# Sum of reciprocals on one core: another command list and a zeroed statistics tile

## The chip, the cores and the metric

The kernel runs on 1 core of one Trainium2 chip. The metric is the device time of one execution in microseconds (us); the median of the runs counts. In the text PE is TensorE, ACT is ScalarE, DVE is VectorE, POOL is GpSimd and SP is SyncE, the names that the profile uses.

## The reference

```python
x = np.abs(np.random.randn(32, 512, 1024)).astype(np.float32) + 1e-6

def reference(x):
    return np.sum(1.0 / x, axis=-1).astype(np.float32)
```

There are 32 x 512 = 16384 sums of 1024 reciprocals each, and 67.1 MB to read.

## The kernel before

Each of the 128 partitions holds 128 of the 16384 sums. A "row" u in the kernel is one of these for all partitions at once: a tile of 128 x 1024 numbers, 512 KB. Rows 0 to 126 are whole; row 127 comes in two halves, the pieces 127 and 128. The input goes through `ring`, a buffer of 46 rows in SBUF; row u lies at place u mod 46, so row 46 can be loaded when row 0 is done with.

The work is written out by hand as a list of commands, `PLAN`. Each engine does its commands in the order in which they stand there; between engines, `note` keeps track of who must wait for whom, row by row. A command is a letter, a row, "+n" for n rows in one instruction, and "@b" for a slot or a bank:

- D n: SP issues the loads of the next n rows (one load, or more at a border of the ring or of the input). It waits until the places in the ring are free.
- A u+n: ACT takes the reciprocal square root of n rows in place. The square of that is the reciprocal, and the sum of the squares is what is wanted.
- The squares are summed in one of several ways. Z: ACT squares and sums (an activation and the reading of its accumulator). Q: DVE squares and sums in one instruction. G and T: POOL squares n rows in place, DVE sums n rows. C and T: ACT squares, DVE sums. B: DVE takes statistics of each half row (count, mean and count times variance, of even and odd numbers); two later commands, K on ACT (the means squared, times the count) and M on DVE (adding up), make sums of them for many rows at once.
- P, U, L, E, R are a way of their own for one row, by pairs: 1/a + 1/b = (a + b) / (a b). P: POOL multiplies the row's two halves into a slot of `prod`. U: PE adds the halves in a bank of PSUM. L and E: ACT takes the reciprocal square root of the products, and squares it. R: DVE multiplies by the sums and adds up.
- O: SP issues six stores of the sums; a last one stands at the end of the program.

Sums go to the tile `sums`, but the statistics of the B rows go to the tile `stats`, which holds only the rows of `STATS` (11 rows from 43 in steps of 3, 18 rows from 80 in steps of 2). K0 and M0 treat the first group, K1 and M1 the second, and M writes its results into `sums` among the others. POOL has 13 idle words (`EARLY`) ahead of its first command.

The list of before has 25 loads; the first four ask for 2, 12, 12 and 9 rows.

Of the kernel before, what the change touches and what calls it, by code (L numbers as in the profile page):

```python
# [11 lines left out]
def kernel(  # L12
# [17 lines left out]
    STATS = ((43, 3, 11), (80, 2, 18),)  # L30
# [3 lines left out]

    PLAN = """
        D2 D12 D12 D9 D11 A0+2 Z0 A2 A3 A4+3 G1+3 A7 A8 A9 G6+3 A10 T1 A11+3 T2+2 Z4 Z5 G9 Z10
        Z12 G11 T6+4 D10 A14 A15+2 G13 A17+3 G16 T11 T13 A20+4 G17 Q15 G19 T16+2 A24+2 G20 A26
        A27 G21 A28+2 G23+3 A30+2 T19+3 A32+3 Z14 D8 G26 C33 Z18 G27 Z22 Z29 G28 A35+2 G30+3
        T23+6 D8 A37+3 A40+4 G34+2 T30+2 A44+2 Z36 T32 G40 Z37 T33+3 D8 Z38 G44+2 U53@0 A46+2
        T40 A48 Q42 G47 A49 A50+3 B43 T44 P53@0 T45 A54+2 G50 B46 L53 T47 Z39 D6 B49 A56+6 T50
        B52 Q54 B55 A62+2 G57 Q56 E53 G60 Z41 D6 R53 Z48 T57 A64+6 B58 G62 T60 G63 B61 T62+2
        A70+2 G65+2 B64 Z51 D7 D6 B67 Z59 D5 G68+2 A72 T65+2 D4 A73+4 B70 G71+2 T68+2 D3 A77+2
        B73 A79 G78 T71+2 D2 K0 U81@1 A80 A82+2 G79 M0 B80 A84 U85@2 B82 P81@1 Z74 D2 T78+2 Z75
        G83 L81 Z76 D2 P85@2 B84 U89@3 A86+3 T83 P89@3 U91@4 P91@4 L85 B86 G87 L89 A90 B88 L91  # L50
        T87 E81 E85 E89 R81 E91 R85 Z77 D1 D1 D1 D1 D1 D1 R89 B90 A92+2 P95@0 U95@5 R91 A94 B92
        G93 L95 B94 A96 A97 T93 A98 B96 E95 B98 Z97 P99@1 U99@6 A100+2 R95 P103@2 L99 B100 G101
        A102 U103@7 L103 B102 A104 T101 E99 E103 R99 P107@3 U107@0 A105 R103 A106 B104 P109@4
        U109@1 L107 Q105 A108 L109 B106 E107 E109 R107 P111@0 U111@2 A110 B108 A112 P113@1 R109
        U113@3 L111 B110 L113 E111 B112 E113 P115@2 U115@4 A114 R111 P116@3 L115 R113 U116@5
        E115 B114 P118@4 A117 R115 U118@6 L116 K1 Q117 L118 E116 P119@0 M1 O0 A120 U119@7 R116
        E118 Q120 L119 E119 P121@1 U121@0 R118 A122 R119 A123 Q122 L121 Q123 A124 E121 Q124 A125
        R121 A126 Q125 A127 A128 Q127 Z126 Q128
# [27 lines left out]
    stat_rows = [i for lo, step, n in STATS for i in range(lo, lo + step * n, step)]  # L86
    stats = pool.tile([P, len(stat_rows), 2, 2, 3], f32)
# [70 lines left out]
    with tc.manual_schedule():  # L158
        for _ in range(EARLY):
            nc.gpsimd.nop(hint="idle", nofuse=True)  # L160
        for op, u, n, b in (parse(tok) for tok in PLAN):
# [23 lines left out]
            elif op == "Z":  # L185
                r = place(u)[0]
                inst = nc.scalar.activation(  # L187
                    out=area(u), in_=area(u), func=Square, accum_out=sums[:, r : r + 1]
                )
                summed.add(r)  # L190
                note("ACT", inst, writes=rows(u))
# [26 lines left out]
            elif op == "R":  # L218
# [9 lines left out]
                    accum_out=sums[:, u : u + 1],  # L228
                )
                note("DVE", inst, [("bank", bank[u])], [("slot", slot[u])])  # L230
            elif op == "Q":
                r, at, w = place(u)
                joined = [u]
                while len(joined) < n:
# [4 lines left out]
                total = sums[:, r : r + 1]  # L239
# [5 lines left out]
                    scalar=total if r in summed else 0.0,  # L245
                    op0=mult,
                    op1=add,
                    accum_out=total,
                )
                summed.add(r)  # L250
                note("DVE", inst, writes=[s for i in joined for s in rows(i)])
            elif op == "B":
                i = stat_rows.index(u)
                for h in range(2):
                    inst = nc.vector.bn_stats(  # L255
                        out=stats[:, i, h], in_=ring[:, u % R, h * H : (h + 1) * H]
                    )
                    note("DVE", inst, reads=half(u, h * H), writes=[("stat", i)])
            elif op in "KM":
                lo, step, n = STATS[u]  # L260
                i = stat_rows.index(lo)
                part = stats[:, i : i + n]
                if op == "K":
                    mean = part[:, :, :, :, 1].rearrange("p f h e -> p (f h e)")
                    inst = nc.scalar.activation(  # L265
                        out=mean, in_=mean, func=Square, scale=float(H // 2) ** 0.5
                    )
                    engine = "ACT"
                else:
                    inst = nc.vector.tensor_reduce(  # L270
                        out=sums[:, lo : lo + step * (n - 1) + 1 : step],
                        in_=part[:, :, :, :, 1:].rearrange("p f h e k -> p f (h e) k"),
                        axis=mybir.AxisListType.XY,
                        op=add,
                    )
                    engine = "DVE"
                note(engine, inst, writes=[("stat", j) for j in range(i, i + n)])
# [4 lines left out]
            elif op == "T":  # L282
                inst = nc.vector.tensor_reduce(  # L283
                    out=sums[:, u : u + n],
# [4 lines left out]
                note("DVE", inst, reads=rows(u, n))  # L289
# [34 lines left out]
```

## Time and profile before

| | |
|---|---|
| median of 3 runs | 166.15 us (166.03 to 166.23) |
| span of the profiled execution, first to last instruction | 164.2 us |
| profiled execution's own time | not given apart from its span; the median stands 1.9 us above the span |
| busy: ACT, DVE, POOL, PE | 145.7, 115.9, 108.8, 38.2 us |
| instructions: ACT, DVE, POOL, PE | 148, 147, 56, 68 matmuls and as many weight loads |
| read from HBM | 67.11 MB, 409 GB/s over the span |
| PE clock granted, mean | 0.952 |

In the rows of the timeline, a group of neighbouring instructions stands with its start, the busy time of the group, engine, line, operation, what it writes and reads, the count, and in brackets how long the engine sat idle before it and what ended that. In the groups by shape there follow, after the count: busy time in us, mean duration of one in ns, and the idle time before them with its releasers. L178 is line 178: A and C; L187 is Z; L211 is L and E; L240 is Q; L220 is R; L255 is B; L265 is K; L270 is M; L280 is G; L283 is T; L194 is P; L201 is U; L170 is a load; L156 is a store.

### The profile page before, as it was taken

How to read it: one execution, taken by the hardware profiler on the slowest of the kernel's cores; microseconds unless marked ns; L12 is line 12 of the kernel's file. 1: busy time of each engine (PE TensorE's matmuls, PEld its weight loads, DVE VectorE, ACT ScalarE, POOL GpSimd, SP SyncE). 2: the span in 40 equal slices, each digit the busy share in tenths (PEclk: the TensorE clock that was granted, in tenths of full speed). 3: DMA queues.
4: the chain of work that ended last, by engine and by line, in shares of the span. 5: the costliest groups of instructions: out<-in, count | busy, mean ns of one | idle time of the engine just before them, and what ended most of it. 6: DMA issues, size and time to landing. Idle time of an engine off the chain costs nothing.

```text
span 164.2 us, 640 instructions
## 1 busy us (share of the span) xinstructions
PE 38.2 (23%) x68; PEld 14.4 (9%) x68; DVE 115.9 (71%) x147; ACT 145.7 (89%) x148; POOL 108.8 (66%) x56
## 2 busy tenths in 40 slices
PE   0000000000000000053000000065908198699700
PEld 0000000000000000020000000032302033234200
DVE  0000003559927039999999999999698969999894
ACT  3600199999999999999999999999999999999994
POOL 1000069998999999999507979999926195477300
PEclk9999999999999999999999999999975859999985
DMA  5999899899989899999998998999999999999970
GB/s 188 463 539 407 383 395 563 383 431 431 463 351 527 351 479 409 391 455 431 391 503 383 431 463 381 455 407 441 419 425 467 414 419 422 421 411 417 408 249 2
DMA packets 4611, 67.20 MB, mean 409 GB/s; under 512 B 1408, under 2 KB 1408, under 8 KB 2176
## 3 DMA queue, kind: packets, MB, share of 16 engines
q1 hardware_dynamic: 4608, 67.18, 96.3%
q14 instruction: 3, 0.02, 0.0%
HBM read 67.11 MB, written 0.07 MB: 409 GB/s over the span
## 4 chain that ended last, share of the span: by engine, by line
ACT 63%; DMA 26%; DVE 6%; issue 2%; POOL 2%; SPq 0%; DVEq 0%; POOLq 0%
ACT ring L178 47%; DMA ring<-in_x_dram 26%; ACT ring L187 10%; ACT prod L211 6%; DVE ring L240 2%; DVE stats L255 2%; POOL prod L194 2%; DVE prod L220 1%; DVE sums L283 0%; SPq L170 0%; ACT stats L265 0%; DVE sums L240 0%; DVE sums L220 0%; DVEq L240 0%; POOLq L194 0%
## 5 line engine op out<-in xcount | busy, mean ns | idle before, releaser
L178 ACT ACTIVATE ring<-ring 128x1024 f32<-128x1024 f32 (+4 forms) x65 | 104.1, 1658 | 15.2 <-DMA ring<-in_x_dram 15.1
L280 POOL TENSOR_TENSOR ring<-ring 128x1024 f32<-128x1024 f32 (+2 forms) x33 | 85.9, 2634 | 29.9 <-ACT ring L178 29.9
L283 DVE TENSOR_REDUCE sums<-ring 128x1 f32<-128x1024 f32 (+4 forms) x27 | 53.3, 1999 | 42.2 <-POOL ring L280 42.1
L201 PE MATMUL ps<-ring,ident 128*128 128x512 f32 x68 | 38.2, 712 | 117.2 <-DMA ring<-in_x_dram 115.9
L255 DVE BATCH_NORM_STATS2 stats<-ring 128x6 f32<-128x512 f32 x58 | 36.5, 679 | 3.1 <-ACT ring L178 3.1
L194 POOL TENSOR_TENSOR prod<-ring 128x512 f32<-128x512 f32 x17 | 22.5, 1339 | 15.0 <-DMA ring<-in_x_dram 10.8
L201 PEld LDWEIGHTS ps<-ring,ident 128*128 128x128 f32 x68 | 14.4, 224 | 140.2 <-POOL ring L280 71.6
L187 ACT ACTIVATE ring<-ring 128x1024 f32<-128x1024 f32 x23 | 23.9, 1041 | 0.0
L211 ACT ACTIVATE prod<-prod 128x512 f32<-128x512 f32 x34 | 19.8, 615 | 0.2
L240 DVE CUSTOM_DVE_ANT_0 ring<-ring 128x1024 f32<-128x1024 f32 (+1 forms) x12 | 17.6, 1480 | 0.5 <-ACT ring L178 0.4
L220 DVE CUSTOM_DVE_ANT_0 prod<-prod,ps 128x512 f32<-128x512 f32 x17 | 11.1, 676 | 0.1
L187 ACT ACTIVATION_READ_ACCUMULATOR ring<-ring 128x1 f32 x23 | 4.3, 187 | 0.0
L70 ACT ACT_TABLE_LOAD x1 | 1.3, 1283 | 0.7 <-PEq L308 0.7
L220 DVE DVE_READ_ACCUMULATOR2_ANT sums<- 128x1 f32 x17 | 1.4, 81 | 0.0
L240 DVE DVE_READ_ACCUMULATOR2_ANT sums<- 128x1 f32 x13 | 1.0, 81 | 0.0
L240 DVE CUSTOM_DVE_ANT_0 ring<-ring,sums 128x512 f32<-128x512 f32 x1 | 0.8, 752 | 0.1
masks.py:199 POOL TENSOR_SCALAR_AFFINE_SELECT ident<-ident 128x128 f32<-128x128 f32 x1 | 0.3, 293 | 0.5 <-POOL ident masks.py:197 0.5
L265 ACT ACTIVATE stats<-stats 128x44 f32<-128x44 f32 (+1 forms) x2 | 0.5, 272 | 0.0
L270 DVE TENSOR_REDUCE sums<-stats 128x11 f32<-128x88 f32 (+1 forms) x2 | 0.5, 264 | 0.0
masks.py:197 POOL MEMSET ident<- 128x128 f32 x1 | 0.2, 205 | 0.3 <-POOLq L308 0.3
L308 POOL MEMSET const-float32-0.0<- 128x1 f32 x1 | 0.1, 99 | 0.2 <-issue 0.2
L308 POOL MEMSET const-bfloat16-1.0<- 128x1 bf16 x1 | 0.1, 102 | 0.0
(2 smaller groups left out, 0.2 us busy)
## 6 DMA issues: line engine op xcount, KB each, us to landing
ring<-in_x_dram SPq DMA_DIRECT2D x2, 6144.0 KB, 25.8
ring<-in_x_dram SPq DMA_DIRECT2D x3, 4096.0 KB, 26.0
ring<-in_x_dram SPq DMA_DIRECT2D x3, 3072.0 KB, 26.3
ring<-in_x_dram SPq DMA_DIRECT2D x1, 5632.0 KB, 55.9
ring<-in_x_dram SPq DMA_DIRECT2D x1, 5120.0 KB, 32.4
ring<-in_x_dram SPq DMA_DIRECT2D x1, 4608.0 KB, 43.3
ring<-in_x_dram SPq DMA_DIRECT2D x4, 1024.0 KB, 37.8
ring<-in_x_dram SPq DMA_DIRECT2D x1, 3584.0 KB, 24.4
```

Source lines behind the costliest of these rows:

```text
L70: nc.scalar.add_instruction(mybir.InstLoadActFuncSet(name=nc.get_next_instruction_name(), act_func_set_id=act_sets.index("abs_reciprocal_s ...
L178: inst = nc.scalar.activation(out=area(u, n), in_=area(u, n), func=Arsqrt if op == "A" else Square, scale=FIT if op == "A" else 1.0,)
L187: inst = nc.scalar.activation(out=area(u), in_=area(u), func=Square, accum_out=sums[:, r : r + 1])
L194: inst = nc.gpsimd.tensor_tensor(out=prod[:, b], in0=ring[:, r, :H], in1=ring[:, r, H:], op=mult)
L201: inst = nc.tensor.matmul(ps[:, b], lhsT=ident, rhs=ring[:, r, h * H : (h + 1) * H], start=h == 0, stop=h == 1,)
L211: inst = nc.scalar.activation(out=pair, in_=pair, func=Arsqrt if op == "L" else Square, scale=S * FIT if op == "L" else 1.0,)
L220: inst = nc.vector.tensor_tensor_reduce(out=pair, in0=pair, in1=ps[:, bank[u]], scale=S, scalar=0.0, op0=mult, op1=add, accum_out=sums[:, ...
L240: inst = nc.vector.tensor_tensor_reduce(out=row, in0=row, in1=row, scale=1.0, scalar=total if r in summed else 0.0, op0=mult, op1=add, acc ...
L255: inst = nc.vector.bn_stats(out=stats[:, i, h], in_=ring[:, u % R, h * H : (h + 1) * H])
L265: inst = nc.scalar.activation(out=mean, in_=mean, func=Square, scale=float(H // 2) ** 0.5)
L280: inst = nc.gpsimd.tensor_tensor(out=row, in0=row, in1=row, op=mult)
L283: inst = nc.vector.tensor_reduce(out=sums[:, u : u + n], in_=area(u, n), axis=mybir.AxisListType.X, op=add,)
```

## The change

The list is another one. It has 26 loads, the first five of 10, 9, 8, 10 and 9 rows, 13 rows by pairs instead of 17, 26 B rows instead of 29, 57 rows by T instead of 47 (55 of them squared by POOL instead of 46), 24 by Z instead of 23, and 9 Q commands instead of 13. No program of an engine is to be over 152 words long. The idle words of POOL are gone.

`stats` now has a place of 12 numbers for each of the rows 0 to 118, and POOL sets it to zero at the start. A row below 119 leaves its sum there, whatever the way: B its twelve numbers, and Z, Q, T and R one number in a place that M adds up. K and M run over all rows of a block (0 to 61, 62 to 118), so that M writes `sums` for every row of the block. Rows from 119 on go to `sums` as before.

```diff
--- before.py
+++ after.py
@@ -18,7 +18,6 @@
     nc = tc.nc
     f32 = mybir.dt.float32
     P = 128
-    EARLY = 13
     D = 1024
     H = D // 2
     F = 128
@@ -27,35 +26,27 @@
     NP = 5
     PIECES = ((127, 0, 512), (127, 512, 512))
     NR = 127
-    STATS = ((43, 3, 11), (80, 2, 18),)
+    BLOCKS = (62, 119,)
     STORES = (0, 21, 43, 64, 81, 99, 116)
     S = float(2**17)
     FIT = 1.0 - 2.0**-17
     PLAN = """
-        D2 D12 D12 D9 D11 A0+2 Z0 A2 A3 A4+3 G1+3 A7 A8 A9 G6+3 A10 T1 A11+3 T2+2 Z4 Z5 G9 Z10
...
+        D10 D9 D8 D10 D9 A0+8 A8+2 G6 Z4 G2 Z5 G0+2 A10 A11+8 G8+2 Z10 G18 Z7 G12 Z13 T18
+        A20 G14+3 A24+3 Z26 A19 A21+3 T14+3 Z11 G22+4 Z20 T12 T1+2 A35 A36 T8+2 A27+7 B3 G19
+        T6 T0 G35 B21 D9 A34 G32 T22+4 C33+2 A37 Z17 G36+2 A38+8 B31 D9 T32+4 G27+4 T19 D8
+        Z45 Z38 A47+8 G39 T27+4 G40+2 T36+2 D6 G42 Z49 G52+3 A46 T39+4 Z48 Z46 A59 A60 B43
+        D8 A61+3 G59+2 T52+3 A55+4 G62 B63 B61 G44 Z56 B47 T62 G50+2 A69+2 T59+2 A64+5 B57
+        G69 G55 Z68 B64 G70 A71+7 B58 T44 G65 T50+2 D6 G66 T55 D5 B67 D6 K0 G72 Z74 D4 D4 M0
+        Z75 B76 G71 Z73 T72 A80+2 G77 T65+2 A82 G80+2 T77 D3 A78+2 T71 A83+3 T69+2 T80+2 D2
+        A90+2 G84+2 D3 D2 B82 A86+4 B79 G91 B78 Z88 B89 D2 P93@0 U93@0 A94+3 T91 G83 B86 L93
+        U92@1 P92@1 T83+3 Z96 G95 L92 Z90 E93 G94 B87 E92 A100+3 D1 U98@2 R93 P99@2 R92
+        T94+2 P98@3 L99 U99@3 E99 P97@4 L98 B100 E98 L97 U97@4 D1 P105@0 B102 A106 R98
+        P103@1 L105 U105@5 B106 A104 G101 E97 R99 L103 U103@6 R97 E105 B104 E103 D1 P108@2
+        A109+2 U107@7 R103 T101 P107@3 L108 B110 E108 G109 L107 E107 R105 D1 U111@0 A112+2
+        R107 P111@4 T109 L111 Q112 D1 A114+2 U108@1 Q113 E111 R108 Z114 B115 A117 D1 P116@0
+        U116@2 R111 A118 B117 L116 B118 E116 P119@1 A120 U119@3 R116 K1 Q120 L119 E119
+        U122@4 A121 P122@2 M1 O0 R119 A123 Q121 L122 Q123 A124 E122 Q124 A125 R122 A126 Q125
+        A127 A128 Q127 Z126 Q128
     """.split()
 
     Arsqrt = mybir.ActivationFunctionType.Abs_reciprocal_sqrt
@@ -83,8 +74,7 @@
     ring = pool.tile([P, R, D], f32)
     sums = pool.tile([P, F], f32)
     prod = pool.tile([P, NP, H], f32)
-    stat_rows = [i for lo, step, n in STATS for i in range(lo, lo + step * n, step)]
-    stats = pool.tile([P, len(stat_rows), 2, 2, 3], f32)
+    stats = pool.tile([P, BLOCKS[-1], 2, 2, 3], f32)
     ident = pool.tile([P, P], f32)
     ps = pspool.tile([P, 8, H], f32)
     make_identity(nc, ident)
@@ -138,6 +128,14 @@
                     (inst, *entry, writing, sum(count.values()), known)
                 )
 
+    def total(u, n=1):
+        if u < BLOCKS[-1]:
+            return stats[:, u : u + n, 0, 0, 2]
+        return sums[:, u : u + n]
+
+    def result(u, n=1):
+        return [("sum", i) for i in range(u, u + n)]
+
     def rows(u, n=1):
         spaces = []
         for r, at, w in (place(i) for i in range(u, u + n)):
@@ -156,8 +154,7 @@
         nc.sync.dma_start(out=out_v[a, :, at : at + hi - lo], in_=sums[:, lo:hi])
 
     with tc.manual_schedule():
-        for _ in range(EARLY):
-            nc.gpsimd.nop(hint="idle", nofuse=True)
+        note("POOL", nc.gpsimd.memset(stats, 0.0), writes=result(0, BLOCKS[-1]))
         for op, u, n, b in (parse(tok) for tok in PLAN):
             if op == "D":
                 n, u = u, loaded
@@ -185,10 +182,10 @@
             elif op == "Z":
                 r = place(u)[0]
                 inst = nc.scalar.activation(
-                    out=area(u), in_=area(u), func=Square, accum_out=sums[:, r : r + 1]
+                    out=area(u), in_=area(u), func=Square, accum_out=total(r)
                 )
                 summed.add(r)
-                note("ACT", inst, writes=rows(u))
+                note("ACT", inst, writes=rows(u) + result(r))
             elif op == "P":
                 slot[u], r = b, u % R
                 inst = nc.gpsimd.tensor_tensor(
@@ -225,9 +222,9 @@
                     scalar=0.0,
                     op0=mult,
                     op1=add,
-                    accum_out=sums[:, u : u + 1],
-                )
-                note("DVE", inst, [("bank", bank[u])], [("slot", slot[u])])
+                    accum_out=total(u),
+                )
+                note("DVE", inst, [("bank", bank[u])], [("slot", slot[u])] + result(u))
             elif op == "Q":
                 r, at, w = place(u)
                 joined = [u]
@@ -236,57 +233,54 @@
                 at -= sum(place(i)[2] for i in joined[1:])
                 w += sum(place(i)[2] for i in joined[1:])
                 row = ring[:, r % R, at : at + w]
-                total = sums[:, r : r + 1]
                 inst = nc.vector.tensor_tensor_reduce(
                     out=row,
                     in0=row,
                     in1=row,
                     scale=1.0,
-                    scalar=total if r in summed else 0.0,
+                    scalar=total(r) if r in summed else 0.0,
                     op0=mult,
                     op1=add,
-                    accum_out=total,
+                    accum_out=total(r),
                 )
                 summed.add(r)
-                note("DVE", inst, writes=[s for i in joined for s in rows(i)])
+                note("DVE", inst, writes=[s for i in joined for s in rows(i)] + result(r))
             elif op == "B":
-                i = stat_rows.index(u)
                 for h in range(2):
                     inst = nc.vector.bn_stats(
-                        out=stats[:, i, h], in_=ring[:, u % R, h * H : (h + 1) * H]
-                    )
-                    note("DVE", inst, reads=half(u, h * H), writes=[("stat", i)])
+                        out=stats[:, u, h], in_=ring[:, u % R, h * H : (h + 1) * H]
+                    )
+                    note("DVE", inst, half(u, h * H), result(u) + [("mean", u)])
             elif op in "KM":
-                lo, step, n = STATS[u]
-                i = stat_rows.index(lo)
-                part = stats[:, i : i + n]
+                lo, hi = ((0,) + BLOCKS)[u : u + 2]
+                part = stats[:, lo:hi]
+                means = [("mean", i) for i in range(lo, hi)]
                 if op == "K":
                     mean = part[:, :, :, :, 1].rearrange("p f h e -> p (f h e)")
                     inst = nc.scalar.activation(
                         out=mean, in_=mean, func=Square, scale=float(H // 2) ** 0.5
                     )
-                    engine = "ACT"
+                    note("ACT", inst, writes=means)
                 else:
                     inst = nc.vector.tensor_reduce(
-                        out=sums[:, lo : lo + step * (n - 1) + 1 : step],
+                        out=sums[:, lo:hi],
                         in_=part[:, :, :, :, 1:].rearrange("p f h e k -> p f (h e) k"),
                         axis=mybir.AxisListType.XY,
                         op=add,
                     )
-                    engine = "DVE"
-                note(engine, inst, writes=[("stat", j) for j in range(i, i + n)])
+                    note("DVE", inst, means + result(lo, hi - lo))
             elif op == "G":
                 row = area(u, n)
                 inst = nc.gpsimd.tensor_tensor(out=row, in0=row, in1=row, op=mult)
                 note("POOL", inst, writes=rows(u, n))
             elif op == "T":
                 inst = nc.vector.tensor_reduce(
-                    out=sums[:, u : u + n],
+                    out=total(u, n),
                     in_=area(u, n),
                     axis=mybir.AxisListType.X,
                     op=add,
                 )
-                note("DVE", inst, reads=rows(u, n))
+                note("DVE", inst, rows(u, n), result(u, n))
             elif op == "O":
                 for lo, hi in zip(STORES, STORES[1:]):
                     store(lo, hi)
```

More of the change, by code (lines that the diff above doesn't have):

```diff
@@ L41 @@
     PLAN = """
-        D2 D12 D12 D9 D11 A0+2 Z0 A2 A3 A4+3 G1+3 A7 A8 A9 G6+3 A10 T1 A11+3 T2+2 Z4 Z5 G9 Z10
[L43 to L58, printed above, removed]
+        D10 D9 D8 D10 D9 A0+8 A8+2 G6 Z4 G2 Z5 G0+2 A10 A11+8 G8+2 Z10 G18 Z7 G12 Z13 T18
```

## The prediction

> **What bounds the kernel now.** I read the page first (busy times, slices, queues, the chain that ended last), then the chain in order of time, the timeline, the DMA answer in short windows, and the groups by shape. The page:
>
> ```profile
> PE 38.2 (23%) x68; PEld 14.4 (9%) x68; DVE 115.9 (71%) x147; ACT 145.7 (89%) x148; POOL 108.8 (66%) x56
> ...
> DMA  5999899899989899999998998999999999999970
> ...
> q14 instruction: 3, 0.02, 0.0%
> ...
> ACT 63%; DMA 26%; DVE 6%; issue 2%; POOL 2%; SPq 0%; DVEq 0%; POOLq 0%
> ```
>
> Two resources are full at once. The DMA engines are busy in every slice from the second to the one before last, so the loads run as one unbroken stream; and ScalarE (ACT) carries most of the chain. The chain in order of time and the timeline say when each led:
>
> ```profile
> 1.17 18.77 DMA ring<-in_x_dram
> ...
> 99.43 24.43 DMA ring<-in_x_dram
> ...
> 161.93 0.01 DVEq L319
> ```
>
> ```profile
> 5.48 1.91 ACT L178 ACTIVATE ring<-ring 128x2048 f32<-128x2048 f32 x1 [3.46 <-DMA ring<-in_x_dram]
> ...
> 19.97 11.09 ACT L178 ACTIVATE ring<-ring 128x1024 f32<-128x1024 f32 x8 [11.40 <-DMA ring<-in_x_dram]
> ...
> 71.59 3.75 PE L201 MATMUL ps<-ring,ident 128*128 128x512 f32 x4 [71.59 <-DMA ring<-in_x_dram]
> ...
> 100.67 7.31 ACT L178 ACTIVATE ring<-ring 128x1024 f32<-128x1024 f32 x4 [0.23 <-DMA ring<-in_x_dram]
> ...
> 108.08 5.18 PE L201 MATMUL ps<-ring,ident 128*128 128x512 f32 x8 [32.73 <-DMA ring<-in_x_dram]
> ...
> 131.20 5.40 PE L201 MATMUL ps<-ring,ident 128*128 128x512 f32 x8 [3.51 <-DMA ring<-in_x_dram]
> ```
>
> The chain led through loads until 19.94 and from 99.43 to 123.86, and between and after them mostly through ACT, to a DVE that has finished at 161.93. Each of these instructions starts as a load lands, so they date the stream: 2 rows landed at 5.48, 14 at 19.97, 56 at 71.59, 80 at 100.67, 86 at 108.08, 105 at 131.20. A row took (19.97 - 5.48) / 12 = 1.2075 us at first and 29.08 / 24 = 1.212 between 56 and 80. But the 42 rows between 19.97 and 71.59 took 1.229 each: at 1.212 they had been there at 70.9. The stream fell back by 0.7 us once. From 80 to 86 it lost 7.41 - 7.27 = 0.14 more. What happened there shows in the DMA answer for 60 to 70, 99 to 105 and 105 to 120 us, the only stretches with this line:
>
> ```profile
> q14 instruction: 1, 0.01, 0.2%
> ...
> q14 instruction: 1, 0.01, 0.3%
> ...
> q14 instruction: 1, 0.01, 0.1%
> ```
>
> Three times an engine's program was fetched through the same DMA engines. Every load is spread over all of them and lands with the slowest. I take the 0.7 + 0.14 us for the price of the fetches: the first one puts one DMA engine back, the others hit other engines and so cost little more. The trace doesn't show this link directly; it is the main doubt below.
>
> **ACT's account.** The durations:
>
> ```profile
> L178 ACT ACTIVATE ring<-ring 128x1024 f32<-128x1024 f32 x36 | 36.4, 1041 | 11.6 <-DMA ring<-in_x_dram 11.6
> ...
> L187 ACT ACTIVATE ring<-ring 128x1024 f32<-128x1024 f32 x23 | 23.9, 1041 | 0.0
> ...
> L211 ACT ACTIVATE prod<-prod 128x512 f32<-128x512 f32 x34 | 19.8, 615 | 0.2
> ...
> L178 ACT ACTIVATE ring<-ring 128x6144 f32<-128x6144 f32 x2 | 10.6, 5308 | 0.0
> ...
> L265 ACT ACTIVATE stats<-stats 128x72 f32<-128x72 f32 x1 | 0.3, 298 | 0.0
> ...
> L265 ACT ACTIVATE stats<-stats 128x44 f32<-128x44 f32 x1 | 0.2, 246 | 0.0
> ```
>
> ```profile
> 147.38 1.27 ACT L211 ACTIVATE prod<-prod 128x512 f32<-128x512 f32 x2
> ...
> 150.23 1.13 ACT L211 ACTIVATE prod<-prod 128x512 f32<-128x512 f32 x2
> ...
> 157.79 3.03 ACT L178 ACTIVATE ring<-ring 128x1024 f32<-128x1024 f32 x4
> ...
> 160.73 1.04 ACT L187 ACTIVATE ring<-ring 128x1024 f32<-128x1024 f32 x1
> ```
>
> A further row in an A costs (5308 - 1041) / 5 = 853 ns. The eight A from 19.97 hold 12 rows in 11.09, so an A itself adds about (11.09 - 12 x 0.853) / 8 = 0.10. A Z costs 1.04; an L or E 0.52 in a row (1.13 for two, the ends overlapping), and 0.12 more where it follows the command that wrote its own operand (L115, E115: 1.27).
>
> Before: 64 A with 111 rows, 6.4 + 94.7; one C 0.95; 23 Z 23.9; 34 L and E 17.7; two K 0.4; 4 such neighbours 0.5: 144.6. Check: at 19.97 ACT had done A0+2 and Z0, 3.0; 19.97 + 141.6 + 0.2 of waits (0.23 at 100.67) = 161.8, and the last Z starts at 160.73 and ends 1.04 later. So ACT is loaded without a gap from 19.97 to the end; what could be gained is ahead of 19.97.
>
> After: 46 A with 115 rows, 4.6 + 98.1; C33+2 1.8; 24 Z 25.0; 26 L and E 13.5; two K over 248 and 228 numbers instead of 44 and 72: by the slope 52 / 28 ns, 0.63 and 0.59, behind others 1.0 together (bounds 0.4 to 2); neighbours (Z26, C33, Z45, Z49, Z56, Z68, Z88, E99, E98, E108, E107, E116, E119) 13 x 0.12 = 1.6. Sum 145.6, 1.0 more than before.
>
> But the first load now has 10 rows and lands once, at 19.97 - 4 x 1.2075 = 15.1. Before, ACT lost 11.4 us ahead of 19.97 after 3 us of work; now it starts at 15.1 and has 10.9 us to do (A0+8, A8+2, Z4, Z5) until the next nine rows land at 26.0. Start plus work: 15.1 + 145.6 = 160.7, plus waits.
>
> **Waits of ACT on loads.** Landings at 1.212 a row without a setback (80 rows at 99.9), then 1.217, as from 108.08 to 131.20; ACT's free time against them: A10 25.97 against 26.0; A35 47.5 against 47.8; A37 58.7, 58.7; A47+8 69.9, 69.6; A69 90.2, 90.2; A80 107.3, 107.3; A90 114.5, 114.5; A94 121.1, 120.7; A100 127.9, 127.9; A106 133.5, 132.9. The two run neck and neck: waits sum to about 0.6, and ACT is behind from A106 on. Z126 would end at 161.3, and A127 begin near 159.2 (before 160.82 - 0.61 - 0.52 = 159.7).
>
> **VectorE (DVE), GpSimd (POOL) and the ring.**
>
> ```profile
> 0.74 147.98 SPq L170 DMA_DIRECT2D ring<-in_x_dram  x25
> ...
> 74.14 2.96 DVE L240 CUSTOM_DVE_ANT_0 ring<-ring 128x1024 f32<-128x1024 f32 x1
> ...
> 75.98 2.25 POOL L194 TENSOR_TENSOR prod<-ring 128x512 f32<-128x512 f32 x1
> ```
>
> ```profile
> L280 POOL TENSOR_TENSOR ring<-ring 128x1024 f32<-128x1024 f32 x24 | 47.2, 1987 | 8.7 <-ACT ring L178 8.7
> ...
> L255 DVE BATCH_NORM_STATS2 stats<-ring 128x6 f32<-128x512 f32 x58 | 36.5, 679 | 3.1 <-ACT ring L178 3.1
> ...
> L194 POOL TENSOR_TENSOR prod<-ring 128x512 f32<-128x512 f32 x17 | 22.5, 1339 | 15.0 <-DMA ring<-in_x_dram 10.8 <-DVE stats L255 2.4 <-DVE sums L283 1.7
> L280 POOL TENSOR_TENSOR ring<-ring 128x3072 f32<-128x3072 f32 x4 | 21.2, 5306 | 20.3 <-ACT ring L178 20.3
> ...
> L283 DVE TENSOR_REDUCE sums<-ring 128x2 f32<-128x2048 f32 x8 | 18.2, 2278 | 0.3 <-POOL ring L280 0.2
> L283 DVE TENSOR_REDUCE sums<-ring 128x1 f32<-128x1024 f32 x15 | 17.9, 1206 | 27.4 <-POOL ring L280 27.4
> ...
> L240 DVE CUSTOM_DVE_ANT_0 ring<-ring 128x1024 f32<-128x1024 f32 x11 | 17.0, 1552 | 0.5 <-ACT ring L178 0.4
> ...
> L220 DVE CUSTOM_DVE_ANT_0 prod<-prod,ps 128x512 f32<-128x512 f32 x17 | 11.1, 676 | 0.1
> ...
> L283 DVE TENSOR_REDUCE sums<-ring 128x3 f32<-128x3072 f32 x2 | 6.7, 3349 | 3.3 <-POOL ring L280 3.3
> ...
> L270 DVE TENSOR_REDUCE sums<-stats 128x18 f32<-128x144 f32 x1 | 0.3, 293 | 0.0
> ...
> masks.py:197 POOL MEMSET ident<- 128x128 f32 x1 | 0.2, 205 | 0.3 <-POOLq L308 0.3
> ```
>
> POOL: 55 rows of G in place of 46 (1.99 alone, 1.77 in threes) and 13 P of 1.34: near 118 us, 10 more than before; it is idle until A0+8 ends at 22.1. DVE: ten more rows of T cost near 11; three B, four R and four Q fewer give back 6 x 0.679, 4 x 0.676 and 4 x 1.55, some 13: about as much work as before. Three places decide.
>
> (a) The first refill, rows 46 to 54, waits for T0, DVE's eighth command: A11+8 ends at 34.05, G18, G12 and G14+3 (1.9, 1.9, 5.3 with a little overlap) at 43.1, T14+3, T12, T1+2, T8+2, B3, T6, T0 (3.35 + 1.21 + 2.28 + 2.28 + 1.28 + 1.21 + 1.21, overlaps off) at 55.4. The first load needed 5.48 - 0.74 - 2.4 = 2.3 us besides its transfer (0.74, SP's first issue), so with row 45 landing at 58.7 the refill must be issued by 56.4. It makes it by 1.0 us, and the stream has no hole. The later refills are issued 5 us and more ahead (rows 86 to 91 after T44 at 100.4, wanted by 105).
>
> (b) P ahead of L late on: P92 ends 125.1, wanted 125.3; P99, P98, P97 131.3 and so on, each 0.2 to 0.6 ahead. No new wait, but little cover: POOL late by 1 us would cost ACT some 0.5.
>
> (c) The end: M1 now adds 57 x 8 = 456 numbers, by 293 ns for 144 between 0.3 and 0.9, 0.6 taken. K1 needs the statistics of B118 (151.1) and its turn on ACT comes at 151.8; K0's come with B58 at 99.3, its turn at 103.7, and M0 behind it holds DVE to about 105, where nothing is due yet. M1 follows Q120 (153.1) and K1 (152.3): 153.7. Behind it are R119 and Q121; A121 ends at 154.5, so Q121 waits for ACT anyway and M1 costs nothing. All sums below 119 hang on it; the six stores, SP's only work behind the loads, have until Q128. The tail A127, Q127, A128, Q128, Z126 is as before and follows A127.
>
> **The rest at nothing.** Zeroing 1428 numbers a partition on POOL is at most 1428 / 128 x 0.205 = 2.3 us, over by 5 us in a queue that is idle until 22; without that cover it would cost those 2.3. The 13 idle words of POOL go from the same idle stretch. 52 matmuls for 68: PE waits for loads. Writing a sum into another tile is the same instruction.
>
> **Sum.** From ACT's unbroken start: -4.9 (15.1 for 19.97) + 4.0 (145.6 of work from there for 141.6) + 0.4 (waits 0.6 for 0.2) = -0.5. The profiled span of 164.2 becomes 163.7; I carry the difference to the median, 166.15, which stands 1.9 above the span: 165.7. The waits hold only if the setback of 0.7 us is gone. It goes if no program is fetched midway: ACT's 148 instructions become 124, DVE's 147 become 128, PE's 136 become 104; POOL's 56 become 57.
>
> **The rivals.**
> 1. The setback stays: one fetch is left (POOL's program loses only its idle words), or it isn't the fetches' doing. Since ACT meets the landings within 0.3 us at A69, A80, A90 and A100, 0.7 us less some slack goes straight through: 165.7 + 0.6 = 166.3. For: no row names whose fetches they were. Against: fetch and setback fall into the same stretch. The Trainium skill (Runtime: NRT & Kernel Launch, section Instruction fetch mechanics) has it that fetching runs beside execution and that a block boundary costs next to nothing; by it the fetches were harmless and this case the rule. The trace speaks against it as far as dates go.
> 2. Slower: the first refill misses its time. It decides if T0 ends after 56.4. If POOL's and DVE's steps of (a), 21 us, run 15% long, T0 ends at 58.6 and the stream has a hole of 2.2 us; ACT waits at A47+8, where it had 0.3 to spare, and the end moves by 1.9: 167.6. For: 1 us of cover on a chain over three engines. Against: those durations are means, and the one stretched P (2.25 for 1.34) ran beside a Q (2.96 for 1.55), and no Q runs now before 140 us. Late P (b) would give 166.2 to 166.7 and belongs here.
> 3. Better: K, M and neighbours cost less than taken, and ACT waits nowhere: 165.2.
>
> **How the numbers follow.** Forecast 0.50, rival 1 0.25, rival 2 0.17, rival 3 0.08. 0.2% is 0.33 us, about what a measurement of this kernel can tell from no change. The forecast's own range is 165.4 to 166.0: three quarters of it lie below 165.82. Faster: 0.38 + 0.08 + 0.03 of rival 1; same: 0.12 + 0.12; slower: 0.10 + 0.17. The range from 165.2 to 167.0 leaves out half of rival 2 and part of rival 3.
>
> **What would show it.** Right: ACT's first A at 15.1 and no wait over 0.4 behind it; no q14 line after the start; refill of row 46 issued near 55.4; A127 near 159.2. Wrong: a q14 line and waits of 0.5 at A69 or A80 (rival 1); a stretch with idle DMA engines near 60 (rival 2); L waiting for POOL.

## The result and the profile after

The change makes the kernel slower by 1.3%: 168.16 us (167.72 to 168.67, 4 runs) against 166.09 (165.93 to 166.23, 4 runs), a ratio of 1.0126 [1.0105, 1.0147]. The forecast was 165.7 with a range from 165.2 to 167.0. The profiled execution took 168.28 us with a span of 166.5.

The page of the kernel after:

```profile
PE 26.8 (16%) x52; PEld 10.7 (6%) x52; DVE 113.3 (68%) x128; ACT 147.1 (88%) x124; POOL 118.3 (71%) x57
...
DMA  7899999999999999999999999999999999999940
GB/s 246 384 472 441 425 425 441 441 441 443 423 398 443 416 345 434 434 443 434 434 425 419 431 457 425 415 439 405 442 444 402 435 421 418 424 417 412 409 140 1
...
q14 instruction: 3, 0.02, 0.0%
...
ACT 39%; DMA 32%; DVE 18%; POOL 5%; issue 3%; DVEq 0%
...
L157 POOL MEMSET stats<- 128x1428 f32 x1 | 1.3, 1293 | 0.0
L265 DVE TENSOR_REDUCE sums<-stats 128x62 f32<-128x496 f32 (+1 forms) x2 | 1.3, 638 | 0.0
L260 ACT ACTIVATE stats<-stats 128x248 f32<-128x248 f32 (+1 forms) x2 | 1.0, 518 | 0.0
```

The work is what was forecast: POOL 118.3, K 0.52 each, M 0.64 each, the zeroing 1.3. No slice of the DMA line shows a hole (a slice is 4 us wide, and "9" is 90% or more), but the row of GB/s has a dip to 345 in the slice from 58.3 us on. And DVE, 6% of the chain before, now has 18% of it. The chain in order of time of the kernel after says where DVE comes in:

```profile
0.74 14.75 DMA ring<-in_x_dram
15.51 7.08 ACT ring L175 x2
...
34.45 9.02 POOL ring L274 x3
43.49 8.87 DVE stats L277 x4
52.36 1.19 DVE stats L250 x2
53.55 2.25 DVE stats L277 x2
55.80 1.19 DVE stats L250 x2
56.99 2.26 DVE stats L277
...
62.50 5.46 DVE stats L277 x2
...
67.97 24.07 DMA ring<-in_x_dram
...
101.99 15.08 DMA ring<-in_x_dram
```

It runs through the three POOL commands and the T and B commands of place (a), down to T0, which ends at 55.80. It does not turn to loads there but goes on along DVE to 67.97, when the load of rows 64 to 71 was issued, for which ACT waited until 92.07. That load stood behind the ones asked for earlier for most of its 24.07 us. So DVE's 18% are no measure of what a late refill cost; the waits of ACT have to be read for that. The timeline of the kernel after, SP's and ACT's rows that waited for loads, and the last Z:

```profile
15.51 8.83 ACT L175 ACTIVATE ring<-ring 128x8192 f32<-128x8192 f32 x2 [13.49 <-DMA ring<-in_x_dram]
...
48.23 11.98 ACT L175 ACTIVATE ring<-ring 128x1024 f32<-128x1024 f32 x6 [0.29 <-DMA ring<-in_x_dram]
...
55.89 5.72 SPq L167 DMA_DIRECT2D ring<-in_x_dram  x2
...
71.43 7.03 ACT L175 ACTIVATE ring<-ring 128x8192 f32<-128x8192 f32 x1 [1.04 <-DMA ring<-in_x_dram]
...
92.07 6.27 ACT L175 ACTIVATE ring<-ring 128x2048 f32<-128x2048 f32 x2 [0.17 <-DMA ring<-in_x_dram]
...
117.09 5.42 ACT L175 ACTIVATE ring<-ring 128x2048 f32<-128x2048 f32 x2 [0.70 <-DMA ring<-in_x_dram]
...
162.80 1.04 ACT L184 ACTIVATE ring<-ring 128x1024 f32<-128x1024 f32 x1
```

The refill of rows 46 to 54 was issued at 55.89, half a us inside the limit of 56.4 that the prediction had set. Yet A47+8 waited 1.04 for it. The windows answer for 56 to 64 us (busy time of PE, PEld, DVE, ACT and POOL, the granted clock, the DMA share, GB/s), of before and then of after:

```profile
56.00:64.00 8.00, 0.00 (x0) 0.00 (x0) 4.03 (x1) 8.00 (x10) 8.00 (x4) 1.00 0.98 423
```

```profile
56.00:64.00 8.00, 0.00 (x0) 0.00 (x0) 8.00 (x6) 7.97 (x7) 6.22 (x4) 1.00 0.94 359
```

A share of 0.94 looks full; the 359 GB/s tell that the stream is short of 8 x (423 - 359) = 0.51 MB, a row of the ring. The trace's records of single DMA packets say how both can be. In after, the 16 DMA engines stood idle for only 0.09 us each between 57 and 66 us; but 23 packets of the refill, all begun between 58.0 and 62.0, took 1.4 to 2.96 us, where the same 36 KB take 1.36 us in an unbroken stream. That adds 0.85 us to each engine's work on average. So the "hole" of this text is mostly a slow start of the refill, with engines that count as busy.

ACT's account, from its start to the end of the last Z, as forecast, in after and in the kernels of the new list on which the argument rests, described below (the waits are those the timeline names; the rest holds the work and the small gaps that it doesn't name):

| | start | named waits | rest | Z126 ends |
|---|---|---|---|---|
| forecast | 15.1 | 0.6 | 145.6 | 161.3 |
| after | 15.51 | 2.20 | 146.1 | 163.84 |
| e1 | 15.55 | 0.47 | 146.2 | 162.19 |
| e2 | 15.68 | 0.29 | 146.1 | 162.09 |
| e7 | 15.44 | 0.91 | 146.0 | 162.33 |
| e10 | 15.48 | 1.27 | 146.1 | 162.88 |
| e12 | 15.48 | 5.32 | 146.1 | 166.94 |

In before, the last Z ends at 160.73 + 1.04 = 161.77; 163.84 - 161.77 = 2.07, as much as the medians differ. The miss against the forecast, 2.5 us, is 0.4 of start, 0.5 of rest and 1.6 of waits.

### The profile page after: what moved, and what is told of

It reads as the page before. It is cut to its first block, busy times and chain, and to the rows that moved or that the text cites. A ratio compares the mean times of both kernels' runs of the same rounds, so it can differ in the third digit from the quotient of the medians.

```text
span 166.5 us, 537 instructions
## 1 busy us (share of the span) xinstructions
PE 26.8 (16%) x52; PEld 10.7 (6%) x52; DVE 113.3 (68%) x128; ACT 147.1 (88%) x124; POOL 118.3 (71%) x57
## 4 chain that ended last, share of the span: by engine, by line
ACT 39%; DMA 32%; DVE 18%; POOL 5%; issue 3%; DVEq 0%
DMA ring<-in_x_dram 32%; ACT ring L175 27%; DVE stats L277 12%; ACT prod L208 8%; POOL ring L274 5%; ACT ring L184 4%; DVE stats L250 4%; DVE ring L236 2%; DVE prod L217 0%; ACT stats L260 0%; DVE sums L236 0%; DVEq L236 0%; DVE sums L217 0%; DVEq L313 0%
## 5 line engine op out<-in xcount | busy, mean ns | idle before, releaser
L175 ACT ACTIVATE ring<-ring 128x1024 f32<-128x1024 f32 (+7 forms) x47 | 106.9, 2315 | 15.7 <-DMA ring<-in_x_dram 15.7
L274 POOL TENSOR_TENSOR ring<-ring 128x1024 f32<-128x1024 f32 (+3 forms) x37 | 99.7, 2724 | 29.2 <-ACT ring L175 29.2
L277 DVE TENSOR_REDUCE stats<-ring 128x1 f32<-128x1024 f32 (+3 forms) x30 | 64.0, 2170 | 46.3 <-POOL ring L274 46.3
L198 PE MATMUL ps<-ring,ident 128*128 128x512 f32 x52 | 26.8, 668 | 130.5 <-DMA ring<-in_x_dram 130.5
L250 DVE BATCH_NORM_STATS2 stats<-ring 128x6 f32<-128x512 f32 x52 | 32.6, 680 | 3.8 <-ACT ring L175 3.7
L191 POOL TENSOR_TENSOR prod<-ring 128x512 f32<-128x512 f32 x13 | 17.0, 1318 | 9.0 <-DMA ring<-in_x_dram 9.0
L198 PEld LDWEIGHTS ps<-ring,ident 128*128 128x128 f32 x52 | 10.7, 214 | 145.9 <-issue 137.2
L208 ACT ACTIVATE prod<-prod 128x512 f32<-128x512 f32 x26 | 15.4, 617 | 0.2
L236 DVE CUSTOM_DVE_ANT_0 ring<-ring 128x1024 f32<-128x1024 f32 (+1 forms) x8 | 9.1, 1157 | 0.0
L217 DVE CUSTOM_DVE_ANT_0 prod<-prod,ps 128x512 f32<-128x512 f32 x13 | 8.7, 678 | 0.5 <-ACT prod L208 0.3
```

The lines of the kernel that those rows point to most:

```text
L175: inst = nc.scalar.activation(out=area(u, n), in_=area(u, n), func=Arsqrt if op == "A" else Square, scale=FIT if op == "A" else 1.0,)
L191: inst = nc.gpsimd.tensor_tensor(out=prod[:, b], in0=ring[:, r, :H], in1=ring[:, r, H:], op=mult)
L198: inst = nc.tensor.matmul(ps[:, b], lhsT=ident, rhs=ring[:, r, h * H : (h + 1) * H], start=h == 0, stop=h == 1,)
L208: inst = nc.scalar.activation(out=pair, in_=pair, func=Arsqrt if op == "L" else Square, scale=S * FIT if op == "L" else 1.0,)
L217: inst = nc.vector.tensor_tensor_reduce(out=pair, in0=pair, in1=ps[:, bank[u]], scale=S, scalar=0.0, op0=mult, op1=add, accum_out=total(u),)
L236: inst = nc.vector.tensor_tensor_reduce(out=row, in0=row, in1=row, scale=1.0, scalar=total(r) if r in summed else 0.0, op0=mult, op1=add, ...
```

## The experiments

Theory H: the refill comes too late for the stream, though not by the prediction's sum. Its rivals: the statistics tile costs the time; the fetches do; the later start does. Of the lists only the stretch that changed is shown; "..." stands for commands that stay.

**e1, the refill 1 us earlier.** T12, which has nothing to do with rows 0 to 8, goes behind T0.

```diff
-  Z20 T12 T1+2 A35 A36 T8+2 A27+7 B3 G19 T6 T0 G35
+  Z20 T1+2 A35 A36 T8+2 A27+7 B3 G19 T6 T0 T12 G35
```

> The changed kernel with one command moved: T12, which the refill of rows 46 to 54 does not need, stands behind T0 instead of ahead of T1+2, so that the refill is issued 1.1 us earlier, near 54.8 instead of 55.9. Theory H (the refill came too late and left a hole in the stream of loads): ACT's wait at A47+8 falls from 1.13 to 0.3 or less and the time to 167.0 to 167.4. Theory F (the hole is of no account, the loss is the program fetches that are still there and the later first landing): time unchanged, 168.0 to 168.3, with the lost wait turning up at the next landings.

Measured: 166.80 us (166.64 to 167.12, 7 runs), ratio 1.0039 [1.0027, 1.0051]. The timeline and then the window of e1:

```profile
54.82 6.84 SPq L167 DMA_DIRECT2D ring<-in_x_dram  x2
...
115.43 5.42 ACT L175 ACTIVATE ring<-ring 128x2048 f32<-128x2048 f32 x2 [0.18 <-DMA ring<-in_x_dram]
```

```profile
56.00:64.00 8.00, 0.00 (x0) 0.00 (x0) 8.00 (x6) 7.97 (x7) 6.22 (x4) 1.00 1.01 433
```

The engines' columns are those of after, the stream is full, and A47+8 and A69 wait no more. By the packet records none of the refill's packets took over 1.4 us. The place of one command was worth 1.36 us, more than expected.

**e2, the refill 19 us earlier.** All that frees the places of rows 0 to 8 goes ahead of G12 and T18.

```diff
-  G18 Z7 G12 Z13 T18 ... Z20 T12 T1+2 A35 A36 T8+2 A27+7 B3 G19 T6 T0 G35
+  G18 Z7 B3 T6 T1+2 T0 T8+2 G12 Z13 T18 ... Z20 T12 A35 A36 A27+7 G19 G35
```

> The changed kernel with B3, T6, T1+2, T0 and T8+2 moved ahead of T18, into the time when DVE has nothing to do, so that the refill of rows 46 to 54 is issued near 37 instead of 55.9, far ahead of its need. H: no hole at all; A47+8 waits 0.1 or less; 166.8 to 167.2, what is left being the later first landing (0.4) and a setback of 0.7 by a fetch at A90. F: 168.0 to 168.3.

Measured: 166.65 (166.52 to 166.92, 10 runs), 1.0029 [1.002, 1.0039], a little under what was expected. The timeline of e2:

```profile
15.68 8.83 ACT L175 ACTIVATE ring<-ring 128x8192 f32<-128x8192 f32 x2 [13.66 <-DMA ring<-in_x_dram]
...
36.66 0.33 SPq L167 DMA_DIRECT2D ring<-in_x_dram  x1
...
48.42 11.97 ACT L175 ACTIVATE ring<-ring 128x1024 f32<-128x1024 f32 x6 [0.29 <-DMA ring<-in_x_dram]
```

These are all its waits: ACT is loaded from 15.68 to the end, and still the kernel is 0.3% slower than before. H holds for 1.5 of the 2.07 us. What is left is that ACT starts 4.29 us earlier than its unbroken run in before (15.68 for 19.97) and has 4.55 us more to do from there.

**e3, the first load split.** After, with two rows asked for first.

```diff
-  D10 D9 D8 D10 D9 A0+8
+  D2 D8 D9 D8 D10 D9 A0+8
```

> The changed kernel with the first load of 10 rows split in one of 2 and one of 8 rows; ACT still begins with A0+8 when both are there. The first landing of ten rows was 15.5 and not 15.1 as forecast. If it is the large first load that starts slowly, ACT begins at 15.1 and the time falls by 0.4 to 167.8; if the stream itself needs that long to start, ACT begins at 15.5 as before and the time stays at 168.2.

Measured: 167.51 (166.87 to 168.53, 6 runs), 1.0094 [1.0065, 1.0123], under both of its forecasts, 167.8 and 168.2. The profile is of the fastest of these runs, 166.87. The timeline of e3:

```profile
15.27 8.83 ACT L175 ACTIVATE ring<-ring 128x8192 f32<-128x8192 f32 x2 [13.25 <-DMA ring<-in_x_dram]
...
55.61 5.71 SPq L167 DMA_DIRECT2D ring<-in_x_dram  x2
...
70.35 7.03 ACT L175 ACTIVATE ring<-ring 128x8192 f32<-128x8192 f32 x1 [0.24 <-DMA ring<-in_x_dram]
```

ACT starts 0.24 earlier, and by that the refill goes out 0.28 earlier, whereupon the wait at A47+8 falls from 1.04 to 0.24: most of the gain is a smaller hole. The spread of 1.7 us between runs, where e2 has 0.4, says that this refill stands at an edge. The start itself is settled by more kernels than this: ACT begins at 15.48 to 15.68 in the six profiled with a ten-row load (after, e1, e2, e5, e10, e12) and at 15.25 to 15.44 in the five with the split (e3, e7, e9, e11, and e8 by its second command).

**e4, the tile alone.** Before, its list and its idle words kept, with the zeroed tile.

```diff
-    STATS = ((43, 3, 11), (80, 2, 18),)
+    BLOCKS = (74, 116,)
...
+        note("POOL", nc.gpsimd.memset(stats, 0.0), writes=result(0, BLOCKS[-1]))
```

> One part of the change alone: the list of before with its 13 idle words and its loads, but with the zeroed statistics tile (blocks 0 to 73 and 74 to 115). Theory H and F alike: the tile costs nothing, 166.0 to 166.3. Rival T (writing the sums into the strided tile, zeroing it, or the longer K and M cost time by themselves): 166.5 or more, with ACT or DVE groups longer than in before.

Measured: 166.27 (166.16 to 166.44, 10 runs), 0.9999 [0.999, 1.0009]. The tile, its zeroing and the longer K and M cost nothing that can be told from no change (0.1% is 0.17 us); that rival is out.

**e5 and e6, whose fetches they are.** e5 is after with idle words at the head of three programs; e6 is before without its idle words.

```diff
+        for _ in range(10):
+            nc.scalar.nop(hint="idle", nofuse=True)
+        for _ in range(27):
+            nc.vector.nop(hint="idle", nofuse=True)
+        for _ in range(30):
+            nc.gpsimd.nop(hint="idle", nofuse=True)
```

> The changed kernel with idle words ahead of each engine's first command: 10 on ACT, 27 on DVE, 30 on POOL. In the changed kernel the three fetches come at 82.9, 110.2 and 143.9 us, when ACT had done 50 instructions, DVE 50 and POOL 70. Theory W (an engine fetches once, at a fixed word of its own program, and these three are ACT's, DVE's and POOL's): the dates become about 69 (ACT's 40th), 82 (DVE's 23rd) and 97 (POOL's 40th). If a fetch belongs to another engine or does not go by words, its date stays where it was. A setback of the slowest DMA engine should move with the dates.

```diff
-    EARLY = 13
+    EARLY = 0
```

> The other part of the change alone: the kernel before without POOL's 13 idle words. If POOL's is one of its three fetches, that one comes later by what POOL needs for 13 instructions (20 us or more), the other two stay. Time 166.0 to 166.4 under every theory, as the first fetch sets the stream back already; more than 166.5 would mean that the idle words were worth something to the kernel before.

Measured: e5 167.54 (a single run), with fetches at 64.58, 75.45 and 97.81 where after has them at 82.9, 110.2 and 143.9; e6 166.47 (166.27 to 166.66, 10 runs), 1.0019 [1.0010, 1.0029], with fetches at 65.8, 99.4 and 146.1 where before has them at 65.8, 100.2 and 112.1. In e5 three programs got words and all three dates moved; in e6 POOL's program lost words and one date moved by 34 us, the other two by less than 1. So the three fetches are those of ACT, DVE and POOL, and shorter programs only put them off. Which of the first two is ACT's and which DVE's is argued from the counts of instructions done. That a fetch stands at a fixed word is not shown: of the dates expected for e5, 69, 82 and 97, the first two came 4 to 7 us early. Counted in the traces, idle words and semaphore instructions included, ACT had done 47 to 51 instructions, DVE 47 to 51 and POOL 70 or 71 at their fetches in every kernel of the new list. With the list of before POOL's count was 63, without its idle words 71, and in e4 DVE's fetch moved from 100.2 to 112 or later though it got no idle words. In e5 the wait of 0.70 at A90 is gone with the fetch at 110, and A47+8 waits 1.00 as in after. e6 came out just above its expectation: in its profile the A at 100.90 waits 0.40 for its load where before has 0.23, and an L at 145.31 waits 0.46 for POOL. Why is not settled.

**e7, both cures.** e2 and e3 together.

```diff
-  D10 D9 D8 D10 D9 A0+8 ... G18 Z7 G12 Z13 T18 ... A35 A36 T8+2 A27+7 B3 G19 T6 T0 G35
+  D2 D8 D9 D8 D10 D9 A0+8 ... G18 Z7 B3 T6 T1+2 T0 T8+2 G12 Z13 T18 ... A35 A36 A27+7 G19 G35
```

> The kernel with the early refill, and its first load split in 2 and 8 rows as well: two causes taken away at once. H: the gains add, ACT begins at 15.2 to 15.3 instead of 15.7 and does not wait on loads but for 0.3, time 166.2 to 166.3 (166.65 less 0.4), level with the kernel before. If the early start is lost again in waits for the stream, 166.6.

Measured: 166.73 (166.69 to 166.83, 5 runs), 1.004 [1.0027, 1.0054]: no better than e2, and above both of its forecasts. The timeline of e7:

```profile
15.44 8.83 ACT L175 ACTIVATE ring<-ring 128x8192 f32<-128x8192 f32 x2 [13.42 <-DMA ring<-in_x_dram]
...
91.00 6.27 ACT L175 ACTIVATE ring<-ring 128x2048 f32<-128x2048 f32 x2 [0.37 <-DMA ring<-in_x_dram]
...
115.58 5.42 ACT L175 ACTIVATE ring<-ring 128x2048 f32<-128x2048 f32 x2 [0.26 <-DMA ring<-in_x_dram]
```

ACT won 0.24 at the start over e2 and waited 0.62 more, at A69 and A90.

**e8, ACT begins at 5.5 us.** e7, with the first two rows as a command of their own.

```diff
-  A0+8 A8+2 G6
+  A0+2 A2+6 A8+2 G6
```

> As the kernel with the early refill and the split first load, and A0+8 done as A0+2 and A2+6, so that ACT begins when two rows are there (5.5) and has 1.8 us less to do at 15.2, for 0.1 us of one more command. If ACT's account sets the end, the time falls by up to 1.7 more, to 164.6; if the stream is the limit (last piece landing at about 160.1, then A128, Q128 and the store), ACT starts to wait on landings again and the time stays at 165.8 to 166.1. I expect the second.

Measured: 166.76 (166.62 to 166.98, 5 runs), 1.0044 [1.0032, 1.0057], where 165.8 to 166.1 was expected. The timeline of e8:

```profile
5.54 1.91 ACT L175 ACTIVATE ring<-ring 128x2048 f32<-128x2048 f32 x1 [3.52 <-DMA ring<-in_x_dram]
15.25 7.12 ACT L175 ACTIVATE ring<-ring 128x6144 f32<-128x6144 f32 x2 [7.80 <-DMA ring<-in_x_dram]
...
26.17 7.98 ACT L175 ACTIVATE ring<-ring 128x1024 f32<-128x1024 f32 x2 [1.73 <-DMA ring<-in_x_dram]
...
91.05 6.27 ACT L175 ACTIVATE ring<-ring 128x2048 f32<-128x2048 f32 x2 [0.53 <-DMA ring<-in_x_dram]
```

Nearly two us of work were done early, and 1.73 of waiting came back at A10. After the last wait, at 91.05, ACT works for 71.1 us without a gap, so the landing of the load with row 70 sets the end. An earlier ACT can't help while the list has that much work behind row 70.

**e9, is the setback the fetches'?** e7 with the idle words of e5.

> The kernel with the early refill and the split first load, plus the idle words of the run before (10 on ACT, 27 on DVE, 30 on POOL), which put the fetches at about 64.6, 75.5 and 97.8 instead of 81.3, 109.5 and 142.5. Without the idle words the loads land 0.6 later for the slowest DMA engine from the landing of 72 rows on (91.0, where ACT waits at A69), and not yet at 64 rows (80.85). Theory W (that step is the price of the fetch before it): the step moves ahead to the landing of 64 rows, about 81.4 (70.0 to 70.5 for 55 rows), and stays 91.0 for 72. Rival: the step belongs to the load or the place in the list and stays at 72 rows. The time stays at 166.6 to 166.8 under both, since the step is only earlier.

Measured: 166.77 (166.71 to 166.82, 4 runs), 1.0042 [1.0027, 1.0057]. The DMA answer for 60 to 70 us has, in e9, the line below and in e7 none; for 80 to 85 e7 has one packet and e9 none. The timeline of e9 follows:

```profile
q14 instruction: 2, 0.02, 0.4%
```

```profile
70.55 7.03 ACT L181 ACTIVATE ring<-ring 128x8192 f32<-128x8192 f32 x1 [0.42 <-DMA ring<-in_x_dram]
...
91.19 6.27 ACT L181 ACTIVATE ring<-ring 128x2048 f32<-128x2048 f32 x2 [0.17 <-DMA ring<-in_x_dram]
```

With two of the fetches moved from 81.3 and 109.5 to 63.6, the first wait of this kind moved from A69 to A47+8, which in e7 does not wait. Each load leaves sixteen landing marks in the trace, one for each DMA engine's part. In e9 two of them, 70.31 and 70.53, lie 0.5 us and more behind the other fourteen of the load with row 54, as many as there were fetches ahead of it; in e7 the last comes at 69.94. In before, with one fetch ahead of it, at 65.8, the load that lands next has a single mark behind the rest, at 71.46, where the latest of the others is 70.85. So the setback is the fetch's: about 0.6 us on one DMA engine for each fetch, and a load lands with the slowest. Moving it did not change the time.

**e10 and e12, the refill still later.** After, with T0 two commands and then a whole group later.

```diff
-  T6 T0 G35 B21 D9 A34
+  T6 G35 B21 T0 D9 A34
```

> The suspected cost doubled: in the changed kernel T0 stands behind B21, so that the refill of rows 46 to 54 is issued 1.2 us later still, near 57.1. H: past the edge each further us of delay is a further us of hole: A47+8 waits 2.2 to 2.5 instead of 1.13 and the time is 169.2 to 169.5. If the wait at A47+8 is taken up by slack further on, the time stays under 168.6.

```diff
-  T6 T0 G35 B21 D9 A34 G32 T22+4 C33+2
+  T6 G35 B21 A34 G32 T22+4 T0 D9 C33+2
```

> The changed kernel with T0, and with it the refill of rows 46 to 54, behind T22+4: issued near 61.4, 2.3 us after row 45 has landed, so that the stream is empty for certain. Issued at 54.8 the refill left no hole, at 55.9 one of 1.3 us in the landing of 55 rows, at 57.0 one of 1.0. Theory D (a refill into an empty stream costs its whole way, as the first load: 15.5 - 0.7 = 14.7 for ten rows, 13.5 for nine): landing at about 74.9, 4.9 late, A47+8 waits 4.6, time 170.5 to 171.5. Theory S (the price is a fixed one of about 1.2 us as soon as the stream has been let run out, and the date counts little): landing by 72, time 168 or less.

Measured: e10 167.38 (166.91 to 167.75, 4 runs), 1.0072 [1.0046, 1.0098]; e12 171.43 (171.38 to 171.55, 4 runs), 1.0327 [1.0309, 1.0344]. The timelines of e10 and of e12:

```profile
56.99 4.59 SPq L167 DMA_DIRECT2D ring<-in_x_dram  x2
...
71.17 7.03 ACT L175 ACTIVATE ring<-ring 128x8192 f32<-128x8192 f32 x1 [0.81 <-DMA ring<-in_x_dram]
```

```profile
61.31 0.80 SPq L167 DMA_DIRECT2D ring<-in_x_dram  x2
...
74.61 7.03 ACT L175 ACTIVATE ring<-ring 128x8192 f32<-128x8192 f32 x1 [4.25 <-DMA ring<-in_x_dram]
```

e12 came as the theory of an empty stream says: 74.61 - 61.31 = 13.3 us from issue to the ninth row, 11 of them transfer; the 2.4 that are left agree with the prediction's 2.3 for a load into an empty stream. e10 did not: issued 1.1 us later than after, it waited less. H in its simple form, a us of hole for a us of delay, fell. What stands is an edge and a price behind it that is not even:

| refill issued | 36.66 (e2) | 54.82 (e1) | 55.61 (e3) | 55.89 (after) | 56.99 (e10) | 61.31 (e12) |
|---|---|---|---|---|---|---|
| wait at A47+8 | none | none | 0.24 | 1.04 | 0.81 | 4.25 |
| DMA engines idle, mean of one | 0.0 | 0.0 | 0.03 | 0.09 | 0.15 | 4.17 |
| longer packets, mean of one engine | 0.0 | 0.0 | 0.2 | 0.85 | 0.4 | 0.6 |

The last two rows are from the packet records between 57 and 66 us (longer packets: what the refill's packets took over 1.36 us each). They say where after lost more than e10, in packets of up to 2.96 us where e10's took at most 1.94, but not why.

**e11, less for ACT.** e7, with row 88 squared and summed by DVE instead of ACT.

```diff
-  B78 Z88 B89 D2
+  B78 B89 Q88 D2
```

> The kernel with the early refill and the split first load, and row 88 squared and summed by DVE (Q88 behind B89) instead of ACT (Z88): ACT has 1.04 us less to do behind its last wait on the stream, DVE 1.14 us more, where it has gaps of 0.34 and 0.26. If ACT alone sets the end, 165.7; if DVE, which waits for ACT's results by only a few tenths from 143 us on, becomes the bound, 166.3 to 166.6. I expect the second, 166.4.

Measured: 167.47 (167.38 to 167.63, 4 runs), 1.0079 [1.0064, 1.0094], where 166.4 was expected. The timeline of e11 (its A94+3, P93, Q88, G83 and L92), and the row of G83 in e7:

```profile
121.55 2.76 ACT L175 ACTIVATE ring<-ring 128x3072 f32<-128x3072 f32 x1 [0.68 <-DMA ring<-in_x_dram]
121.59 1.27 POOL L191 TENSOR_TENSOR prod<-ring 128x512 f32<-128x512 f32 x1 [0.53 <-DMA ring<-in_x_dram]
...
122.10 1.84 DVE L236 CUSTOM_DVE_ANT_0 ring<-ring 128x1024 f32<-128x1024 f32 x1
...
122.82 2.88 POOL L274 TENSOR_TENSOR ring<-ring 128x1024 f32<-128x1024 f32 x1
...
126.95 0.63 ACT L208 ACTIVATE prod<-prod 128x512 f32<-128x512 f32 x1 [1.08 <-POOL prod L191]
```

```profile
122.95 1.90 POOL L274 TENSOR_TENSOR ring<-ring 128x1024 f32<-128x1024 f32 x1
```

Q88 and G83 both came out long (a Q late in after takes 1.22), so P92 came late and ACT waited for POOL: the prediction's place (b). The dates look as if POOL and DVE had taken turns: P93 ends at 122.86, Q88 1.08 behind that, and G83 1.76 behind Q88. This is read from one place and not tested. ACT's shorter work shows in its account, 144.9 instead of 146.0, but its waits rose from 0.91 to 2.64: 1.08 for POOL, and 0.65 more on loads, at A69 and A94+3. In all it costs 0.74 us over e7, where the prediction gave 0.5 for a us of POOL. No version of the new list beats before.

## Why the prediction was wrong, point by point

- **Place (a), the first refill: the step that failed.** The dates were right: T0 ends at 55.80 against 55.4, the issue at 55.89. The limit was wrong. The 2.3 us that a load needs besides its transfer came from the very first load, and 56.4 from it. That is the price of a load into an empty stream, and e12 bears it out (2.4); it was taken for the lead that keeps a running stream whole. e1 and e3 put the limit between 54.82 and 55.61. The last landing mark of row 45 is at 59.19 in e1 and 58.86 in e3, so 4.4 us ahead of it were enough here and 3.3 were not; in after, where the mark is at 59.14, the lead was 3.3 too. The wait that the prediction put at nothing was 1.04 us at A47+8, and the whole refill cost 1.4 to 1.5 us by e1 and e2. What rival 2 forecast came about without its condition, a T0 later than 56.4 by steps 15% long; and its sign, idle DMA engines near 60, hardly showed, for the engines were busy with longer packets. Why a refill issued 2.1 (e10) to 3.3 us ahead starts so slowly stays open.
- **The setback: rival 1's mechanism came true, its price did not.** The prediction took shorter programs for programs without a fetch. Three fetches are left in every kernel here, e5 and e6 show that they are ACT's, DVE's and POOL's, and e9 that a fetch puts one DMA engine back by about 0.6 us. Rival 1 gave 0.6 us for that. Of the kernels without a hole, e7 waits 0.91 where 0.6 was forecast with the setback gone, but e2 only 0.29, with the same fetches; so the price lay between nothing and 0.3 here, where ACT starts 0.3 to 0.6 later than forecast and so meets the landings later. The Trainium skill (Runtime: NRT & Kernel Launch, section Instruction fetch mechanics) has instructions fetched in blocks of 256 beside execution, mostly hidden. The traces agree in part: ACT has no wait at 82.9 in after, so nothing stops on the engine, but the loads land later, and programs of 124 and 128 counted instructions fetch midway.
- **The start: mis-sized by 0.4.** 10 rows land at 15.49 instead of 15.1. Split in two loads (e3) it is 0.24 earlier; in after the slowest DMA engine finished the ten rows at 15.49 and the median one at 15.02.
- **ACT's work: mis-sized by 0.5,** 146.1 instead of 145.6, and 146.0 to 146.2 in all the kernels of the table, so not a matter of the named waits. In which commands it lies was not taken apart.
- **Account without the hole:** 165.7 + 0.3 to 0.6 of start + 0.4 to 0.5 of work - 0.3 to + 0.3 of waits gives e2 (166.65) and e7 (166.73). That part alone turns the forecast gain of 0.5 into a loss of 0.5 to 0.7.
- **Right:** the tile at nothing (e4); K 0.1 below its estimates and M within 0.05 of them; POOL's 118; (b) and (c): no L waits for POOL in after, and M1 is hidden. Right too that ACT and the stream run neck and neck. The start's gain, booked at 4.9 us, was had at 4.3 to 4.5, and in e2 ACT then waits only 0.29 in all. That is about as far as it goes: e7 and e8 show that a still earlier start is handed back at the next landings.

## What to carry to other kernels

A refill must be queued well before the transfer ahead of it ends, and that lead is to be taken from a refill in the middle of a stream, not from the latency of the first load; here 4.4 us were enough and 3.3 were not. The busy share of the DMA engines did not show this loss (0.94 in after); the GB/s beside it did (359 for 423). When the busiest engine and the load stream end together, cost an edit on both, for what one gains ahead of the other comes back as a wait. A dependency chain over three engines is cheaply tested by moving one command that the awaited one does not need, as T12 here.

## What the runs showed of the hardware

- The price of a late refill is not even: issues at 55.61, 55.89, 56.99 and 61.31 cost A47+8 0.24, 1.04, 0.81 and 4.25 us, and at the edge runs scatter by 0.8 to 1.7 us where e2 and e12 scatter by 0.2 to 0.4. In after the loss lay in the refill's packets up to 62 us, which took up to 2.96 us for 1.36 (0.85 us for each engine), and hardly in idle engines (0.09 us each). Why 55.89 is worse than 56.99 stays open; one profile of each is too little where runs scatter so.
- ACT, DVE and POOL each fetch once midway, and earlier with idle words at the head of their programs (64.6, 75.5 and 97.8 in e5 for 82.9, 110.2 and 143.9). A fetch puts one of the sixteen DMA engines back by about 0.6 us (71.46 against 70.85 in before); it shows as ACT waiting for a load some us later, where ACT is early enough.
- DVE's square-and-sum and POOL's square at the same time took 1.84 and 2.88 us, against 1.22 and 1.90 apart (one pair, in e11).
